# A one-core encoder trunk: input loads issued at once, constants on TensorE first, other banks for k and v, weights through ScalarE's queue, and a smaller share of gathers

## The chip, the core and the metric

One core of a Trainium2 chip runs the whole layer in one launch. Its engines are TensorE (PE; PEld is its loading of stationary operands), VectorE (DVE), ScalarE (ACT), GpSimd (POOL) and SyncE (SP), which issues most transfers. The metric is the device time of one execution, in microseconds (us); the median of several runs counts.

## The reference, cut

One layer over 512 tokens of width 1024: an input projection feeds a differential attention and a two-way gated recurrence (RG-LRU), then a layer with product keys that picks 8 x 16 of 16384 single-neuron experts per token, then a gated embedding, and a last norm.

```python
xn = rms_norm(h, norm_mix_g); proj = xn @ w_in          # q, k, v, lru_in, lru_gate
attn = rms_norm(diff_attention(q, k, v, lam, positions), diff_norm_g)
rec = rms_norm(bi_rglru(lru_in, lru_gate, ...), lru_norm_g)
h = h + concat(attn, rec) @ w_out
xn = rms_norm(h, norm_ffn_g)
ue = exp_u[ib]; logits = einsum('td,tkd->tk', xb, ue)   # 128 experts per token
act = gelu(logits) * gb
ve = exp_v[ib]; h = h + einsum('tk,tkd->td', act, ve)
h = h + sigmoid(rms_norm(h, norm_ple_g) @ ple_w_gate) * (p @ ple_w_proj)
out = rms_norm(h, final_norm_g)
```

## The kernel before

The 512 tokens are four tiles t of 128. Every large product is made of three matmuls (`mm3`, L94): both factors are split into a high and a low part (`split`, L87: ScalarE rounds the high part, L88, VectorE subtracts for the low part, L90 or L92). A scheduler orders each engine's instructions from the order of the code and the waits between them; each engine then runs its own in that order.

**Start.** `x_load` (L183) loads xT in four pieces of two k tiles into `xr`, a ring "w" of three buffers that it shares with the weights; `lru_w` (L175) loads and splits one column tile `ct` of the projection for the recurrence. `x_norm` (L195) loads the four blocks of `h` and takes their squares; `psr` (L278) spreads the resulting `rstd` over the partitions. Then 8 column tiles run over `ct`.

**q, k, v.** The loop at L386 makes three blocks of columns (q, k, v). Each block takes four banks `pst` of the pool `mm` (four buffers), one for each t, so a block can begin only when ScalarE has emptied the banks of the block before (`xn`, L417). Alongside run pieces of the recurrence and its output (`psq`, L360; `psb`, L373; `wo`, L341). After it come the turns `pt` of the attention (L453).

**The experts.** Token tiles 0 to 2 are done densely: the U sweep takes 128 steps over j, each loads a tile of `u`, splits it (`rh`, `rl`) and makes 24 matmuls 128x384 into one of two banks `psl` (`u_mm`, L642), which ScalarE turns into `lg` or, in the last 26 steps, into `keep`. `builds` (L941) makes the matrix of routing weights `gd` in HBM in the background. The V sweep takes 128 steps of 18 matmuls 128x512 into six banks `acc`; its stationary operand is `am` = `lg` times `gc`, the weights of eight steps at a time (`weights`, L981; eight parts a chunk), split into `ah` and `al` (`v_prep`, L1034). `settle` (L989) opens the pools of the V sweep and loads the first chunk of `gc` when the weights are done.

Token tile 3 is done by gathers: 128 rows of `u` and 128 rows of `v`, each one indirect transfer by GpSimd and one VectorE instruction (`rows`, L887; u L913, v L920). `Background.run` paces them: a step gives it a share (`SIDE_1`, `SIDE`, `SIDE_2`, in the V sweep `BG_V`) and a row costs 1.15; what is left runs behind the V sweep. `behind` (L874) places an instruction after the last split made so far.

**End.** `finish(t)` (L1106): norm of `h` (`x`, L1112), turn, split (`hl`), the gate's matmuls (`gate`), sigmoid (L1129), `sg`, `h` (L1130, L1131), last norm (L1141) and store. For t=3 it needs the last gathered row.

Of the kernel before, what the change touches and what calls it, by code (L numbers as in the profile page):

```python
# [39 lines left out]
KEEP = 26  # L40
G_SCALE = 2.0 ** 14
RO_AT = [2, 1, 1, 1, 1, 1, 1, 0, 0, 1, 0, 0, 1, 0, 0, 1, 0, 0, 1, 1, 9]
TOP_FIRST, TOP_THEN, MAKE, SIDE_1, SIDE, BG_V, HOT_DVE, PREP, SIDE_2 = 2.2, 1.0, 0.5, 0.6, 1.2, 1.2, 4, 60, 2.1
LAST = 3
N_AT = 15, 17, 17


# [11 lines left out]
def trunk(ctx, tc, x, xT, pT, pos, w_lru, w_qkv, w_out, w_q, keys, wab, w_gate, w_proj,  # L59
# [85 lines left out]
    with ExitStack() as st:  # L145
# [26 lines left out]
        xgh = ra.tile([P, DK, T], R, name="xgh")  # L172
        xgl = ra.tile([P, DK, T], R, name="xgl")

        def lru_w(ct):  # L175
            w = wr.tile([P, DK, P], F32, tag="w", name="w", bufs=3)
            nc.sync.dma_start(w, w_lru[ct])
            wh = wr.tile([P, DK, P], R, tag="wh", name="wh")
            wl = wr.tile([P, DK, P], R, tag="wl", name="wl")
            split(w, wh, wl)  # L180
            return wh, wl

        def x_load(k2):  # L183
            xr = wr.tile([P, 2, T], F32, tag="w", name="xr", bufs=3)
            nc.sync.dma_start(xr, xT[2 * k2 * P:2 * (k2 + 1) * P, :].rearrange("(k p) t -> p k t", p=P))
            for kk in range(2):
                k = 2 * k2 + kk
                split(xr[:, kk, :], xgh[:, k, :], xgl[:, k, :], scale=col(C_MIX + k))

        x_load(0)  # L190
        wnext = lru_w(0)
        for k2 in range(1, 4):
            x_load(k2)

        def x_norm():  # L195
            for t in range(NT):
# [188 lines left out]

        for blk in range(3):  # L386
            accs = []
            for t in range(NT):
                pst = mm.tile([P, T], F32, tag="mm", name="pst")
                accs.append(pst)  # L390
            for k2 in range(4):
                w2 = wr.tile([P, 2, T], F32, tag="w", name="w2", bufs=3)
# [585 lines left out]
        while feed and len(ahead) < 3:  # L978
            ahead.append(row_load(feed.pop(0)))

    def weights(c, part, vp):  # L981

        if part == 0:
            gcs.append(vp.tile([P, NTB, JC, TB], F32, tag="gc", name="gc"))
        b0, b1 = part * NTB // JC, (part + 1) * NTB // JC
        j = order[c * JC]
        nc.sync.dma_start(gcs[-1][:, b0:b1], gd[b0:b1, :, j * TB:(j + JC) * TB].rearrange("b p (j t) -> p b j t", t=TB))

    def settle():  # L989

        e0.close()
        vp_ = vx.enter_context(tc.tile_pool(name="vp", bufs=2, side="right", reuse_waits="tile"))
        wt_ = wx.enter_context(tc.tile_pool(name="wt", bufs=1, reuse_waits="tile"))
        psv = sv.enter_context(tc.tile_pool(name="psv", bufs=1, space=PSUM, reuse_waits="tile"))
        accs_ = [[psv.tile([P, T], F32, name=f"acc{t}{n}") for n in range(2)] for t in range(ND_V)]
        for part in range(JC):
            weights(0, part, vp_)
        return vp_, wt_, accs_

    vx = ctx.enter_context(ExitStack())  # L1000
# [3 lines left out]
    for j in range(P):  # L1004
# [21 lines left out]
        make.run(MAKE)  # L1026
        if make.done and vp is None:
            vp, wt, acc = settle()
        side.run(SIDE_1 if first else SIDE if not make.done else SIDE_2)
    if vp is None:  # L1030
        make.run(1e9)
        vp, wt, acc = settle()
# [1 line left out]
    def v_prep(i):  # L1034
        j = order[i]
        gj = gcs[i // JC][:, :, i % JC, :]
        lg = kept.get(j)
        if lg is None:
            lg = up.tile([P, NU], F32, tag="lg", name="lg")
            nc.sync.dma_start(lg, ld[j])  # L1040
        if i + JC < P:
            weights(i // JC + 1, i % JC, vp)
        am = vp.tile([P, NTB, TB], F32, tag="am", name="am", bufs=1)
        nc.vector.tensor_mul(am, lg.rearrange("p (b t) -> p b t", t=TB), gj)  # L1044
        am = am.rearrange("p b t -> p (b t)")
        ah = vp.tile([P, NV], R, tag="ah", name="ah", bufs=LAST)
        al = vp.tile([P, NV], R, tag="al", name="al", bufs=LAST)
        split(am, ah, al)
        return ah, al
# [230 lines left out]
```

## Time and profile before

| | us |
|---|---|
| runs | 1506.84, 1513.0, 1511.9 |
| median | 1511.9 |
| the profiled execution, own time | 1509.5 |
| its span | 1507.7 |
| PE busy | 1462.2 |
| DVE busy | 1257.5 |
| ACT busy | 741.0 |

The span is what the engines' rows cover; the profiled execution's own time has 1.8 us more. Rows of a timeline give the start from the span's beginning, the length, the engine, the line, and in brackets how long the engine stood idle before and what ended that. PEclk is the granted clock of TensorE, as a share of the higher of its two levels (1.2 and 2.4 GHz).

### The profile page before, as it was taken

The numbers are of one execution on the slowest core, as the hardware profiler recorded it, in microseconds if no ns is written. First come the engines' busy times: TensorE is split into PE (matmuls) and PEld (weight loads), VectorE is DVE, ScalarE is ACT, GpSimd is POOL, SyncE is SP. The second block draws the span as 40 slices with busy tenths as digits, with TensorE's granted clock in tenths as the row PEclk, the third lists the DMA queues.
The fourth block names the chain that finished last, engine by engine and source line by source line (L and its number), as shares of the span: only waits on it lengthen the run. The fifth ranks groups of instructions, "written<-read, shape, count | busy, mean of one in ns | idle before, by whom it ended". The sixth has DMA issues, their size and how long they took to land.

```text
span 1507.7 us, 22152 instructions
## 1 busy us (share of the span) xinstructions
PE 1462.2 (97%) x7881; PEld 1291.0 (86%) x7881; DVE 1257.5 (83%) x2480; ACT 741.0 (49%) x1058; POOL 414.7 (28%) x320
## 2 busy tenths in 40 slices
PE   7999999999999999999999988999999999999997
PEld 5887668899899999999999986888888778888876
DVE  6686896689999999999778767878897578888896
ACT  6974664253555654565455532333333443333446
POOL 0000000011223263233334344344443014344450
PEclk9999999999999999999999999999999999999999
DMA  7133022157689898889998899989999789999962
GB/s 256 56 98 126 1 74 98 43 185 245 226 288 335 286 355 320 312 296 345 370 331 297 269 323 331 317 299 310 353 363 355 237 274 346 352 375 362 357 211 80
DMA packets 169054, 394.19 MB, mean 261 GB/s; under 512 B 15344, under 2 KB 90864, under 8 KB 165872
## 3 DMA queue, kind: packets, MB, share of 16 engines
q1 hardware_dynamic: 112192, 207.52, 41.0%
q0 software_dynamic: 38464, 140.00, 26.2%
q10 hardware_dynamic: 18288, 45.27, 7.8%
q8 instruction: 61, 1.00, 0.3%
q14 instruction: 49, 0.40, 0.1%
HBM read 345.41 MB, written 47.32 MB: 260 GB/s over the span
## 4 chain that ended last, share of the span: by engine, by line
PE 57%; DVE 20%; DMA 9%; issue 7%; ACT 4%; POOL 1%; SPq 1%; DVEq 0%; ACTq 0%; POOLq 0%
PE psl L95 8%; PE psl L97 8%; PE psl L96 8%; PE acc L97 6%; PE acc L96 6%; PE acc L95 6%; DMA r<-in_v_dram 5%; DVE rl L90 4%; DVE rr L913 2%; PE pg L842 2%; PE ps L95 2%; PE ps L97 2%; PE ps L96 2%; DVE h L920 2%; DMA gc<-gd 1%
## 5 line engine op out<-in xcount | busy, mean ns | idle before, releaser
L88 ACT ACTIVATE rh<-r 128x1024 fp32r<-128x1024 f32 x256 | 270.7, 1059 | 418.2 <-PE psl L96 175.2
L90 DVE TENSOR_TENSOR rl<-r,rh 128x1024 fp32r<-128x1024 f32 x256 | 312.2, 1220 | 103.8 <-ACT rh L88 103.0
L95 PE MATMUL psl<-x2h,rh 128*128 128x384 f32 x1024 | 347.6, 340 | 7.1 <-ACT keep L647 4.7
L97 PE MATMUL psl<-x2h,rl 128*128 128x384 f32 x1024 | 343.7, 336 | 3.1 <-DVE rl L90 3.1
L96 PE MATMUL psl<-x2l,rh 128*128 128x384 f32 x1024 | 343.3, 335 | 0.0
L95 PE MATMUL acc<-rh,ah 128*128 128x512 f32 x768 | 300.0, 391 | 3.4 <-ACT ah L88 3.4
L97 PE MATMUL acc<-rh,al 128*128 128x512 f32 x768 | 300.8, 392 | 1.4 <-DVE al L90 1.4
L96 PE MATMUL acc<-rl,ah 128*128 128x512 f32 x768 | 300.1, 391 | 0.9 <-DVE rl L90 0.9
L881 POOL DMA_INDIRECT rr<-in_u_dram,qidx x84 | 122.3, 1456 | 376.9 <-DVE rl L90 177.0
L95 PEld LDWEIGHTS psl<-x2h,rh 128*128 128x128 f32 x1024 | 192.7, 188 | 8.6 <-ACT keep L647 5.1
L97 PEld LDWEIGHTS psl<-x2h,rl 128*128 128x128 f32 x1024 | 192.8, 188 | 4.0 <-DVE rl L90 4.0
L881 POOL DMA_INDIRECT rr<-in_v_dram,qidxv x82 | 138.9, 1694 | 198.9 <-DVE rl L90 172.9
L96 PEld LDWEIGHTS psl<-x2l,rh 128*128 128x128 f32 x1024 | 192.9, 188 | 0.0
L95 PEld LDWEIGHTS acc<-rh,ah 128*128 128x128 f32 x768 | 145.0, 189 | 33.7 <-ACT ah L88 4.0
L97 PEld LDWEIGHTS acc<-rh,al 128*128 128x128 f32 x768 | 144.8, 189 | 33.5 <-DVE al L90 3.4
L96 PEld LDWEIGHTS acc<-rl,ah 128*128 128x128 f32 x768 | 144.7, 188 | 32.1 <-DVE rl L90 1.8
L88 ACT ACTIVATE ah<-am 128x384 fp32r<-128x384 f32 x128 | 66.3, 518 | 108.3 <-DVE am L1044 84.1
L913 DVE CUSTOM_DVE_ANT_0 rr<-rr,xn 128x1024 f32<-128x1024 f32 x84 | 102.1, 1217 | 5.0 <-DMA rr<-in_u_dram,qidx 5.0
L920 DVE SCALAR_TENSOR_TENSOR h<-rr,qg,h 128x1024 f32<-128x1024 f32 x82 | 104.9, 1280 | 1.4 <-DMA rr<-in_v_dram,qidxv 1.4
L881 POOL DMA_INDIRECT xn<-in_u_dram,qidx x44 | 70.0, 1590 | 112.4 <-DVE rl L90 94.1
L881 POOL DMA_INDIRECT xn<-in_v_dram,qidxv x46 | 72.1, 1568 | 99.5 <-DVE rl L90 91.8
L845 ACT COPY sg<-pg 128x512 f32<-128x512 f32 x96 | 95.9, 1109 | 1.0 <-DMA r<-in_ut_dram 0.2
(340 smaller groups left out, 2271.5 us busy)
## 6 DMA issues: line engine op xcount, KB each, us to landing
r<-in_ut_dram SPq DMA_DIRECT2D x128, 512.0 KB
r<-in_v_dram SPq DMA_DIRECT2D x128, 512.0 KB
gd<-sg ACTq DMA_DIRECT2D x24, 1024.0 KB
gc<-gd SPq DMA_DIRECT2D x128, 192.0 KB
ld<-lg ACTq DMA_DIRECT2D x102, 192.0 KB
lg<-ld SPq DMA_DIRECT2D x102, 192.0 KB
w<-in_w_qkv_dram SPq DMA_DIRECT2D x12, 512.0 KB
w<-in_w_lru_dram SPq DMA_DIRECT2D x8, 512.0 KB
```

The lines of the kernel that those rows point to most:

```text
L88: nc.scalar.activation(hi, src, AF.Copy, scale=1.0 if scale is None else scale)
L90: return nc.vector.tensor_sub(lo, src, hi.bitcast(F32))
L95: nc.tensor.matmul(ps, lhsT=lh, rhs=rh, start=first, stop=False)
L96: nc.tensor.matmul(ps, lhsT=lh, rhs=rl, start=False, stop=False)
L97: nc.tensor.matmul(ps, lhsT=ll, rhs=rh, start=False, stop=last)
L842: nc.tensor.matmul(pg[:, i - q, :], lhsT=o1[:, i // 2, :, i % 2], rhs=o2[part][:, i // 2, :, i % 2], start=part == 0, stop=part == 1)
L845: nc.scalar.copy(sg[:, :, s0:s0 + 4].rearrange("p j t -> p t j"), pg)
L881: g = nc.gpsimd.indirect_dma_start(out=dst, out_offset=None, in_=table, in_offset=bass.IndirectOffsetOnAxis(ap=idx, axis=0))
L913: behind(nc.vector.tensor_tensor_reduce(rr, rr, xn[:, t, :], 1.0, 0.0, ALU.mult, ALU.add, act[:, k % 16:k % 16 + 1]))
L920: behind(nc.vector.scalar_tensor_tensor(h[:, t, :], rr, qg[:, t, k:k + 1], h[:, t, :], op0=ALU.mult, op1=ALU.add))
```

## The change

Five things. (1) `x_load` loads straight into `av`, a tile of its own, and the first column tile's weights come in two halves with two pieces of x behind each; SyncE issues all of it with nothing to wait for. (2) `N_HOT`, 13 matmuls of a constant tile on itself, stand first on TensorE. (3) Two of the banks of k are taken from the pool `psb` ("ro", "po"), and two of v ("tr"). (4) The first chunk of `gc`, eight transfers, is issued by ScalarE, and the first `am` is placed behind the split of V row 2. (5) `SIDE_2`, the share of gathers between `settle` and the end of the U sweep, is 0.6 in the place of 2.1.

```diff
--- before.py
+++ after.py
@@ -40,8 +40,9 @@
 KEEP = 26
 G_SCALE = 2.0 ** 14
 RO_AT = [2, 1, 1, 1, 1, 1, 1, 0, 0, 1, 0, 0, 1, 0, 0, 1, 0, 0, 1, 1, 9]
-TOP_FIRST, TOP_THEN, MAKE, SIDE_1, SIDE, BG_V, HOT_DVE, PREP, SIDE_2 = 2.2, 1.0, 0.5, 0.6, 1.2, 1.2, 4, 60, 2.1
+TOP_FIRST, TOP_THEN, MAKE, SIDE_1, SIDE, BG_V, HOT_DVE, PREP, SIDE_2 = 2.2, 1.0, 0.5, 0.6, 1.2, 1.2, 4, 60, 0.6
 LAST = 3
+N_HOT = 13
 N_AT = 15, 17, 17
 
 
@@ -172,25 +173,32 @@
         xgh = ra.tile([P, DK, T], R, name="xgh")
         xgl = ra.tile([P, DK, T], R, name="xgl")
 
-        def lru_w(ct):
+        def lru_w(ct, parts=1):
             w = wr.tile([P, DK, P], F32, tag="w", name="w", bufs=3)
-            nc.sync.dma_start(w, w_lru[ct])
             wh = wr.tile([P, DK, P], R, tag="wh", name="wh")
             wl = wr.tile([P, DK, P], R, tag="wl", name="wl")
-            split(w, wh, wl)
+            for i in range(parts):
+                c = slice(i * DK // parts, (i + 1) * DK // parts)
+                nc.sync.dma_start(w[:, c, :], w_lru[ct][:, c, :])
+                split(w[:, c, :], wh[:, c, :], wl[:, c, :])
+                if parts > 1:
+                    x_load(2 * i)
+                    x_load(2 * i + 1)
             return wh, wl
 
         def x_load(k2):
-            xr = wr.tile([P, 2, T], F32, tag="w", name="xr", bufs=3)
+
+            xr = av[:, 2 * k2:2 * k2 + 2, :]
             nc.sync.dma_start(xr, xT[2 * k2 * P:2 * (k2 + 1) * P, :].rearrange("(k p) t -> p k t", p=P))
             for kk in range(2):
                 k = 2 * k2 + kk
                 split(xr[:, kk, :], xgh[:, k, :], xgl[:, k, :], scale=col(C_MIX + k))
 
-        x_load(0)
-        wnext = lru_w(0)
-        for k2 in range(1, 4):
-            x_load(k2)
+
+        hot = psb.tile([P, T], F32, tag="tr", name="hot", bufs=2)
+        for _ in range(N_HOT):
+            nc.tensor.matmul(hot[:, 0:P], lhsT=ones, rhs=ones, start=True, stop=True)
+        wnext = lru_w(0, 2)
 
         def x_norm():
             for t in range(NT):
@@ -385,8 +393,13 @@
 
         for blk in range(3):
             accs = []
+
             for t in range(NT):
-                pst = mm.tile([P, T], F32, tag="mm", name="pst")
+                tag = ((), ("ro", "po"), ("tr", None, None, "tr"))[blk][t:t + 1]
+                if tag and tag[0]:
+                    pst = psb.tile([P, T], F32, tag=tag[0], name="pst", bufs=2 if tag[0] == "tr" else 1)
+                else:
+                    pst = mm.tile([P, T], F32, tag="mm", name="pst")
                 accs.append(pst)
             for k2 in range(4):
                 w2 = wr.tile([P, 2, T], F32, tag="w", name="w2", bufs=3)
@@ -978,13 +991,13 @@
         while feed and len(ahead) < 3:
             ahead.append(row_load(feed.pop(0)))
 
-    def weights(c, part, vp):
+    def weights(c, part, vp, queue=nc.sync):
 
         if part == 0:
             gcs.append(vp.tile([P, NTB, JC, TB], F32, tag="gc", name="gc"))
         b0, b1 = part * NTB // JC, (part + 1) * NTB // JC
         j = order[c * JC]
-        nc.sync.dma_start(gcs[-1][:, b0:b1], gd[b0:b1, :, j * TB:(j + JC) * TB].rearrange("b p (j t) -> p b j t", t=TB))
+        queue.dma_start(gcs[-1][:, b0:b1], gd[b0:b1, :, j * TB:(j + JC) * TB].rearrange("b p (j t) -> p b j t", t=TB))
 
     def settle():
 
@@ -994,7 +1007,8 @@
         psv = sv.enter_context(tc.tile_pool(name="psv", bufs=1, space=PSUM, reuse_waits="tile"))
         accs_ = [[psv.tile([P, T], F32, name=f"acc{t}{n}") for n in range(2)] for t in range(ND_V)]
         for part in range(JC):
-            weights(0, part, vp_)
+
+            weights(0, part, vp_, nc.scalar)
         return vp_, wt_, accs_
 
     vx = ctx.enter_context(ExitStack())
@@ -1026,7 +1040,7 @@
         make.run(MAKE)
         if make.done and vp is None:
             vp, wt, acc = settle()
-        side.run(SIDE_1 if first else SIDE if not make.done else SIDE_2)
+        side.run(SIDE_1 if first else SIDE if vp is None else SIDE_2)
     if vp is None:
         make.run(1e9)
         vp, wt, acc = settle()
@@ -1041,7 +1055,10 @@
         if i + JC < P:
             weights(i // JC + 1, i % JC, vp)
         am = vp.tile([P, NTB, TB], F32, tag="am", name="am", bufs=1)
-        nc.vector.tensor_mul(am, lg.rearrange("p (b t) -> p b t", t=TB), gj)
+        mul = nc.vector.tensor_mul(am, lg.rearrange("p (b t) -> p b t", t=TB), gj)
+        if i == 0:
+
+            behind(mul)
         am = am.rearrange("p b t -> p (b t)")
         ah = vp.tile([P, NV], R, tag="ah", name="ah", bufs=LAST)
         al = vp.tile([P, NV], R, tag="al", name="al", bufs=LAST)
```

**ScalarE where the U sweep ends.** The last `gd` write of the matrix of weights, and what follows it. Before:

```order
L847 DMA gd<-sg 128x2048
L88 ACTIVATE rh<-r 128x1024
L647 ACTIVATE keep<-psl 128x384
L88 ACTIVATE rh<-r 128x1024
L647 ACTIVATE keep<-psl 128x384
L88 ACTIVATE rh<-r 128x1024
L647 ACTIVATE keep<-psl 128x384
L88 ACTIVATE ah<-am 128x384
L88 ACTIVATE rh<-r 128x1024
L647 ACTIVATE keep<-psl 128x384
```

Now:

```order
L860 DMA gd<-sg 128x2048
L89 ACTIVATE rh<-r 128x1024
L1000 DMA gc<-gd 128x3x128 x8
L660 ACTIVATE keep<-psl 128x384 x2
L89 ACTIVATE rh<-r 128x1024 x2
L660 ACTIVATE keep<-psl 128x384
L89 ACTIVATE rh<-r 128x1024
L660 ACTIVATE keep<-psl 128x384
L89 ACTIVATE rh<-r 128x1024
L660 ACTIVATE keep<-psl 128x384
L89 ACTIVATE rh<-r 128x1024
```

The eight issues of `gc`, which SyncE had before, stand behind one `rh` and ahead of the next `keep`; `ah` stands behind all of these.

**VectorE at the first `am`.** Before (`ISA` is the u row's product and sum, two rows each):

```order
L90 TENSOR_TENSOR rl<-r,rh 128x1024
L913 ISA rr,act_69<-rr,xn 128x1024
L913 ISA act_69 128x1
L913 ISA rr,act_69<-rr,xn 128x1024
L913 ISA act_69 128x1
L1044 TENSOR_TENSOR am<-lg,gc 128x384
L90 TENSOR_TENSOR rl<-r,rh 128x1024
L913 ISA rr,act_69<-rr,xn 128x1024
L913 ISA act_69 128x1
L90 TENSOR_TENSOR al<-am,ah 128x384
L1044 TENSOR_TENSOR am<-lg,gc 128x384
L90 TENSOR_TENSOR rl<-r,rh 128x1024
```

Now:

```order
L933 SCALAR_TENSOR_TENSOR h<-rr,qg,h 128x1024
L91 TENSOR_TENSOR rl<-r,rh 128x1024 x2
L926 ISA xn,act_69<-xn 128x1024
L926 ISA act_69 128x1
L91 TENSOR_TENSOR rl<-r,rh 128x1024 x2
L926 ISA xn,act_69<-xn 128x1024
L926 ISA act_69 128x1
L91 TENSOR_TENSOR rl<-r,rh 128x1024 x2
L1058 TENSOR_TENSOR am<-lg,gc 128x384
L926 ISA xn,act_69<-xn 128x1024
L926 ISA act_69 128x1
L91 TENSOR_TENSOR al<-am,ah 128x384
```

`am` stood between single splits of rows, with two u rows just ahead of it; now it stands behind a pair of splits that ends with V row 2's, with one u row between the pairs.

**VectorE at the last gathered row** (`h<-rr,qg,h` and `h<-xn,qg,h` are v rows; after the last `rl` of the sweep come 19 of them before and 27 now). Before:

```order
L920 SCALAR_TENSOR_TENSOR h<-rr,qg,h 128x1024
L102 RECIPROCAL sm<-sm 128x1
L920 SCALAR_TENSOR_TENSOR h<-rr,qg,h 128x1024
L1141 SCALAR_TENSOR_TENSOR sg<-h,sm,gains 128x512
L920 SCALAR_TENSOR_TENSOR h<-xn,qg,h 128x1024
L1130 TENSOR_TENSOR sg<-sg,pp 128x512
L1141 SCALAR_TENSOR_TENSOR sg<-h,sm,gains 128x512
L100 TENSOR_SCALAR sm<-sm 128x1
L1131 TENSOR_TENSOR h<-h,sg 128x512
L1130 TENSOR_TENSOR sg<-sg,pp 128x512
L1131 TENSOR_TENSOR h<-h,sg 128x512
```

Now:

```order
L1158 SCALAR_TENSOR_TENSOR sg<-h,sm,gains 128x512
L933 SCALAR_TENSOR_TENSOR h<-rr,qg,h 128x1024
L1147 TENSOR_TENSOR sg<-sg,pp 128x512
L933 SCALAR_TENSOR_TENSOR h<-rr,qg,h 128x1024
L1148 TENSOR_TENSOR h<-h,sg 128x512
L933 SCALAR_TENSOR_TENSOR h<-rr,qg,h 128x1024
L1155 TENSOR_REDUCE sm<-sm 128x1 x2
L933 SCALAR_TENSOR_TENSOR h<-xn,qg,h 128x1024
L101 TENSOR_SCALAR sm<-sm 128x1 x3
L103 RECIPROCAL sm<-sm 128x1 x2
```

Before, two products and sums of gates (`sg<-sg,pp`, `h<-h,sg`) stood behind the last v row; now all those of t=0 to 2 stand ahead of it, and only norms follow until the gates of t=3.

## Rows read from the trace of the kernel before

**Rows 1.** The page, busy us of each engine (share of the span) and its instructions.

```profile
PE 1462.2 (97%) x7881; PEld 1291.0 (86%) x7881; DVE 1257.5 (83%) x2480; ACT 741.0 (49%) x1058; POOL 414.7 (28%) x320
```

**Rows 2.** Windows: stretch, its length, then busy us of PE, PEld, DVE, ACT and POOL with the number of instructions, the granted clock (1.00 is the higher level), the DMA engines' busy share, GB/s.

```profile
116.50:120.00 3.50, 3.50 (x10) 2.73 (x9) 3.50 (x18) 3.50 (x7) 0.00 (x0) 0.52 0.86 276
...
126.50:130.20 3.70, 3.70 (x15) 3.16 (x14) 3.70 (x6) 0.21 (x1) 0.00 (x0) 0.54 0.41 133
...
890.00:900.00 10.00, 5.26 (x23) 4.94 (x22) 7.33 (x12) 3.79 (x6) 3.43 (x3) 0.83 0.84 266
...
917.00:930.00 13.00, 8.15 (x22) 5.77 (x21) 9.65 (x16) 4.93 (x8) 4.90 (x3) 0.74 0.75 259
...
1440.00:1460.00 20.00, 18.83 (x92) 15.46 (x91) 19.44 (x27) 9.18 (x16) 9.47 (x10) 1.00 0.69 215
1460.00:1480.00 20.00, 20.00 (x94) 16.63 (x93) 19.96 (x26) 12.35 (x20) 7.55 (x6) 1.00 0.57 193
```

**Rows 3.** The timeline of the start.

```profile
7.53 0.80 PE L95 MATMUL ps<-xgh,wh 128*128 128x512 f32 x1 [7.53 <-ACT wh L88]
...
13.22 0.63 PE L95 MATMUL ps<-xgh,wh 128*128 128x512 f32 x1
...
14.07 0.40 PE L97 MATMUL ps<-xgh,wl 128*128 128x512 f32 x1
...
19.28 1.06 ACT L198 ACTIVATE gates<-h 128x1024 f32<-128x1024 f32 x1 [0.15 <-DMA h<-in_x_dram]
...
22.26 0.21 ACT L101 ACTIVATE rstd<-rstd 128x4 f32<-128x4 f32 x1
...
23.13 0.71 PE L109 MATMUL psr<-dg,ones 128*128 128x128 f32 x4 [0.57 <-DVE dg L108]
```

**Rows 4.** The timeline between the k and the v block.

```profile
112.35 1.21 DVE L90 TENSOR_TENSOR wl<-w,wh 128x1024 fp32r<-128x1024 f32 x1
...
114.74 2.40 ACT L417 ACTIVATE xn<-pst,rstd 128x512 f32<-128x512 f32 x4
...
115.46 0.50 PE L95 MATMUL pst<-wh,xgh 128*128 128x512 f32 x1 [2.65 <-ACT xn L417]
...
117.37 0.63 PE L95 MATMUL pst<-wh,xgh 128*128 128x512 f32 x1
...
122.62 3.63 PE L360 MATMUL psq<-ones,ugz 128*128 128x2 f32 x32
...
127.92 1.91 PE L453 MATMUL pt<-ident,xn 128*128 128x128 f32 x8
```

**Rows 5.** The waits from 865 to 935: engine and line, what it waited for, us in total, times, longest.

```profile
DVE am L1044 <- DMA r<-in_v_dram: 9.4, 1, 9.4
...
PE psl L95 <- ACT keep L647: 4.7, 1, 4.7
...
PE acc L95 <- ACT ah L88: 3.4, 1, 3.4
```

**Rows 6.** The timelines of ScalarE, SyncE and VectorE where the sweeps meet, one after the other, and SyncE's a chunk later.

```profile
871.65 0.33 ACTq L847 DMA_DIRECT2D gd<-sg  x1
873.69 1.06 ACT L88 ACTIVATE rh<-r 128x1024 fp32r<-128x1024 f32 x1 [2.07 <-PE psl L96]
874.66 0.47 ACT L647 ACTIVATE keep<-psl 128x384 f32<-128x384 f32 x1
878.82 0.47 ACT L647 ACTIVATE keep<-psl 128x384 f32<-128x384 f32 x1
...
893.23 0.52 ACT L88 ACTIVATE ah<-am 128x384 fp32r<-128x384 f32 x1 [9.77 <-DVE am L1044]
...
870.49 14.08 SPq L987 DMA_DIRECT2D gc<-gd  x8
884.66 2.72 SPq L636 DMA_DIRECT2D r<-in_v_dram  x2
...
892.63 0.56 DVE L1044 TENSOR_TENSOR am<-lg,gc 128x384 f32<-128x384 f32 x1 [9.42 <-DMA r<-in_v_dram]
...
930.42 1.97 SPq L987 DMA_DIRECT2D gc<-gd  x4
...
932.96 3.62 SPq L987 DMA_DIRECT2D gc<-gd  x4
```

**Rows 7.** VectorE's timeline around the last v row, then ScalarE's behind that row.

```profile
1474.36 0.68 DVE L1131 TENSOR_TENSOR h<-h,sg 128x512 f32<-128x512 f32 x1
...
1477.48 0.75 DVE L1141 SCALAR_TENSOR_TENSOR sg<-h,sm,gains 128x512 f32<-128x512 f32 x1
1478.14 1.28 DVE L920 SCALAR_TENSOR_TENSOR h<-xn,qg,h 128x1024 f32<-128x1024 f32 x1
1479.34 0.69 DVE L1130 TENSOR_TENSOR sg<-sg,pp 128x512 f32<-128x512 f32 x1
...
1480.62 1.28 ACT L1129 ACT_TABLE_LOAD   x1
1481.92 0.60 ACT L1129 ACTIVATE sg<-gate 128x512 f32<-128x512 f32 x1
```

**Rows 8.** The page's costliest groups: line, engine, operation, tiles, count | busy us, mean ns of one | idle time before them.

```profile
L90 DVE TENSOR_TENSOR rl<-r,rh 128x1024 fp32r<-128x1024 f32 x256 | 312.2, 1220 | 103.8 <-ACT rh L88 103.0
...
L920 DVE SCALAR_TENSOR_TENSOR h<-rr,qg,h 128x1024 f32<-128x1024 f32 x82 | 104.9, 1280 | 1.4 <-DMA rr<-in_v_dram,qidxv 1.4
```

## The prediction

> **What bounds the kernel now.** I read the page's busy shares first [rows 1]: TensorE is busy in 97% of the span, so time is won only where TensorE idles or runs at its lower clock, and lost wherever a new idle stretch opens. Then the windows [rows 2] show where that happens: two dips of the granted clock at the change from the k to the v projection, and two gaps at the meeting of the sweeps (890 to 900: TensorE busy 5.26 of 10 us at 0.83; 917 to 930: 8.15 of 13 at 0.74). The last two windows show another limit: from 1440 to 1480 VectorE is busy 39.4 of 40 us. There the end of the program hangs on VectorE, not on TensorE. The timelines [rows 3, 4, 6, 7] and the waits [rows 5] say who is late in each place. All sums stand against the profiled execution's 1509.5 us; the median of the three runs is 2.4 higher.
>
> **Part 1, the start.** The matmuls of the first column tile take 0.63 us still at 13.22 and 0.40 from 14.07 [rows 3]. A 128x512 matmul takes 0.63 too at 117.37 [rows 4], where the granted clock reads 0.52 [rows 2], so TensorE starts at its lower level, 1.2 GHz, and rises after 6.5 us of work (the first stands at 7.53). Thirteen matmuls on constants before the data could bring that rise forward. But the stretch does not end with these matmuls: `psr` at 23.13 waits for `dg`, that for `rstd` (Sqrt at 22.26), that for the squares of the last x block (19.28). What moves `psr` is when the last block of `h` lands. All input is now issued without the ring of three buffers, 5 MB up to that block as before (four x tiles, two weight tiles, four blocks of `h`, 512 KB each), so it lands somewhat sooner: not at all sooner at worst (gain 0.5, the 0.57 of idle ahead of `psr`), at best 4 (the lower level's cost, 6.5 x (1-0.40/0.63) = 2.4, the 0.57, and 1 by which half a weight tile comes sooner than a whole, an estimate). I take 2.5, since the four squares (1.06 each) still follow one another on ScalarE. Term: -2.5 (-4 to -0.5). If the constants do not raise the clock, nothing else changes, as TensorE then still waits for `psr`.
>
> **Part 2, banks for k and v.** TensorE stood 2.65 us before 115.46, for `xn`, four copies of 2.40 us that empty the banks of k [rows 4]. With other banks it waits for the next `wl` instead, whose split ends at 112.35+1.21 = 113.56: 1.9 us less. After the idle time came 3.5 us at a granted clock of 0.52 [rows 2], that is 1.7 us lost; I count this dip as gone, for the gap falls to 0.75. The second dip (126.5 to 130.2, 0.54, again 1.7) follows 32 tiny `psq` matmuls and a wait for splits; both stay. The eight transposes `pt` that filled that place (1.9) now stand behind the first output matmuls, which cancels against the same work saved later. Term: -3.6. Bounds: -1.5 if the dip comes anyway, -5.5 if the second dip goes too.
>
> **Part 3, the meeting of the sweeps.** What is lost there: 4.74 idle and 1.7 of clock in the first gap, 4.85 and 3.4 in the second, 14.7 us in all [rows 2]. The first is the wait for `keep`, 4.7, and the second for `ah`, 3.4 [rows 5]. Both come from SyncE: its eight `gc` issues hold it from 870.49 for 14.08 us, the first V rows are issued at 884.66, and `am` sits on VectorE in front of the splits that TensorE needs, until 892.63 [rows 6]. The change takes these eight issues to ScalarE's queue and puts the first `am` behind the third V row's split. I count the 14.7 as gone, and add what replaces it.
> (a) The eight issues stand on ScalarE behind `rh` and ahead of `keep` of 874.66. Queued behind them are every `keep` and `rh`. `keep` empties the two psl banks, so TensorE can run one more step, until 878.82, the time of the following `keep`, and then stands until ScalarE is free. Their length is not shown for ScalarE. Nearest rows: the same eight at the same place 14.08; the next eight at 930.42, 1.97+3.62 = 5.59 us. Started at 874.75, where the `rh` of 873.69 ends, they end between 880.3 and 888.8, so the stall is 2 to 10.5, counting 0.5 for `keep`. Since the same transfers run then with fewer gathers beside them, I take 884, a stall of 5.6, and 1.7 of clock behind it, as behind the 4.7 of the first gap.
> (b) At the junction `am` now waits for `rl` of V row 2, whose `rh` needs the buffer of the last U row, so TensorE must have finished the U sweep first: rh 1.06, am 0.56, ah 0.52 [rows 6], rl 1.22 [rows 8], 3.4 us of idle, and 2.5 of clock (1.7 and 3.4 followed the two gaps).
> (c) SyncE still issues seven `gc` of the next chunk ahead of the second V row; I add 2.5 of the old second gap for that (0 to 8).
> Sum: -14.7+7.3+5.9+2.5 = +1 (-9 to +12).
>
> By the Trainium skill, "DMA: Bandwidth & Descriptors", section "Issuing engines are not separate DMA queues", a transfer started by another engine runs on the same 16 engines and interleaves, and moving it saves only the sequencer's issue time, usually small beside the transfer. By that rule (a) would nearly vanish, a total of +2.6 in the place of +9.9. The trace disagrees on the usual smallness: here the issues took 14.08 us [rows 6].
>
> **Part 4, fewer gathers.** SIDE_2 of 0.6 leaves eight rows of token tile 3 undone when the sweeps meet. Counted in the order of VectorE's instructions, 27 v rows follow the last `rl` instead of 19, and three each of the gates' products and sums, and one scaling, now come ahead of the last row. VectorE is full there [rows 2], so each counts: 8 rows at 1.20 (1.28 long, but the instruction behind the row of 1478.14 starts 1.20 after it) = 9.6; three products, three sums and a scaling, 0.69, 0.68 and 0.75 long and 0.08 less each in the same way, 1.8 + 1.8 + 0.7 = 4.3 [rows 7, 8]. The last row moves from 1478.14 by 13.9. Behind it the sigmoid of another tile and its table (1.28+0.60) no longer stand ahead of `x`, of which I count 1.4 as saved, since the table must still be loaded in places. TensorE, which now turns t=3 directly after other gates, will have had no work for over 10 us; after gaps of 2.65 to 4.7 it ran at the lower level for 3.4 us, 1.7 lost, after the second gap 3.4: I add 2.5 to the 13.9 - 1.4. Term: +15 (+12 to +18). The gathers' absence frees some VectorE time near 870 to 885, where it idles anyway (9.4 before `am`), so it is worth nothing beyond part 3.
>
> **Sum.** -2.5-3.6+1+15 = +9.9: 1519.4 for the profiled execution, 1521.8 from the median; I say **1521**.
>
> **Rivals.** *The issues are cheap on ScalarE.* If the eight end by 878.8, (a) is nought: meeting 1-7.3 = -6.3, total +2.6, some 1513, within 0.5%. For it: the second eight took 5.59. Against: the first eight can't read all of gd before its last write, issued at 871.65 [rows 6], has landed. The rule of the Trainium skill quoted in part 3 leads here too. *Faster.* The same mechanism, and the V rows land in time too, (c) 0 and no clock lost at the junction: meeting -14.7+3.4 = -11.3; with the tail at its lower end (+12) and the start and banks at their best (-4, -5.5), -8.8: 1503. It decides at about -7.6. Against it stands the tail: 27 rows of 1.20 cannot be hidden on a full engine. *ScalarE is held as long as SyncE was*, until 888.8: stall 10.5 in place of 5.6, +4.9, and 2 for V rows late after it, total +17: 1529. *The constants do nothing*: 1522 to 1523, since only the first matmuls change.
>
> **How the numbers follow.** A measurement of this kernel tells about 0.5% from no change, that is 1504.3 to 1519.5 counts as the same. Forecast 0.42 (1517 to 1525, some of it under 1519.5); held long 0.13; cheap issues 0.34; faster 0.09; the constants' failure 0.02. Leaving out one in ten below and one above: 1505 to 1531. Faster 0.09, same 0.37, slower 0.54.
>
> **What would show it.** Right: `psr` near 20.6; no TensorE idle time over 1 us between k and v; a TensorE wait of 2 to 10 us for `keep` near 879, with ScalarE's eight `gc` issues before it; 3 to 4 us for `ah` where V starts; no wait near 917; the last v row some 28 us before the end still, with 27 rows after the last `rl`. Wrong: if the wait for `keep` is absent (cheap issues), if a wait for V rows comes back, if VectorE has idle time ahead of the last v row (then part 4 is too large), or if the clock dips in the k/v stretch as before.

## The result, and the profile after

| | before | after |
|---|---|---|
| median of 5 runs | 1512.39 | 1535.59 |
| lowest to highest | 1506.84 to 1517.19 | 1531.33 to 1536.81 |
| the profiled execution | 1509.5 | 1536.38 |
| its span | 1507.7 | 1534.5 |

The ratio is 1.0148, with a 95% interval of 1.0114 to 1.0182: 17 to 28 us slower. The forecast was slower by 9, its range ended at 1531.

The page of the kernel after, busy us of each engine, beside [rows 1]. The work is nearly the same (TensorE's 26 records more are the constants), and the span is longer.

```profile
PE 1470.5 (96%) x7907; PEld 1294.0 (84%) x7907; DVE 1253.2 (82%) x2481; ACT 736.1 (48%) x1057; POOL 387.8 (25%) x320
```

Where the 26.8 us of the two spans lie is seen best between marks that both kernels have, the starts of TensorE's first matmuls of given steps in the trace:

| stretch | before | after | difference | forecast |
|---|---|---|---|---|
| start to the first U matmul | 252.1 | 246.6 | -5.6 | -6.1 |
| U steps 0 to 120 | 605.9 | 606.1 | +0.2 | 0 |
| U step 120 to V step 16 (the meeting) | 116.4 | 117.0 | +0.6 | +1 |
| V steps 16 to 58 | 172.0 | 172.5 | +0.6 | 0 |
| V steps 58 to 124 | 286.0 | 303.1 | +17.1 | 0 |
| V step 124 to the last V matmul | 17.1 | 17.8 | +0.7 | 0 |
| behind it (the tail) | 58.3 | 71.5 | +13.2 | +15 |

One stretch was not in the forecast at all: V steps 58 to 124. The windows of the kernel after (columns as in [rows 2]) show it beside the places that were:

```profile
872.00:880.00 8.00, 0.58 (x4) 0.27 (x2) 0.00 (x0) 0.46 (x2) 0.00 (x0) 0.70 1.13 312
880.00:890.00 10.00, 9.91 (x43) 9.92 (x44) 3.60 (x4) 2.80 (x5) 2.62 (x2) 0.72 0.88 259
...
899.00:903.00 4.00, 0.75 (x4) 0.43 (x3) 2.58 (x3) 1.96 (x3) 1.01 (x1) 0.95 0.44 136
...
1165.00:1180.00 15.00, 7.79 (x32) 5.87 (x32) 6.73 (x9) 5.88 (x8) 1.07 (x2) 0.85 0.78 254
...
1220.00:1260.00 40.00, 35.54 (x145) 27.87 (x145) 28.47 (x38) 17.40 (x23) 8.96 (x8) 0.96 0.78 250
...
1485.00:1506.00 21.00, 14.28 (x64) 11.48 (x62) 21.00 (x26) 10.40 (x19) 10.26 (x8) 0.94 0.69 244
...
120.80:124.40 3.60, 3.60 (x12) 3.02 (x13) 3.57 (x8) 1.72 (x3) 0.00 (x0) 0.53 0.16 23
```

Between k and v (the last row) one dip of the clock is left (0.53), the later of the two of [rows 2]. At the meeting TensorE does nearly nothing from 872 to 880, and for part of the next 10 us it runs at the lower level (0.72). From 1165 to 1180 it is busy 7.79 of 15 us (13.17 in the same window of the kernel before), and from 1220 to 1260 some 4.5 us are idle (0.5 before). From 1485 to 1506 VectorE is busy 21.00 of 21 us, the full engine of [rows 2], now later.

**Start and banks.** The timeline of TensorE, then ScalarE, of the kernel after, in the places of [rows 3]:

```profile
1.15 4.92 PE L200 MATMUL hot<-ones 128*128 128x128 f32 x26 [1.15 <-POOL ones L68]
...
7.52 0.39 PE L98 MATMUL ps<-xgh,wl 128*128 128x512 f32 x1
...
18.02 1.06 ACT L206 ACTIVATE gates<-h 128x1024 f32<-128x1024 f32 x1
...
21.01 0.20 ACT L102 ACTIVATE rstd<-rstd 128x4 f32<-128x4 f32 x1
...
21.87 0.71 PE L110 MATMUL psr<-dg,ones 128*128 128x128 f32 x4 [0.67 <-DVE dg L109]
```

The constants run from 1.15, and the real matmuls take 0.39 from 7.52 on (0.63 still at 13.22 in [rows 3]), but `psr` comes at 21.87 in the place of 23.13: the squares that it needs still come one after the other, the last at 18.02. Between k and v the wait of 2.65 us for `xn` [rows 4] is one of 0.55 for `wl`:

```profile
112.38 0.50 PE L97 MATMUL pst<-wl,xgh 128*128 128x512 f32 x1 [0.55 <-DVE wl L91]
```

**The meeting.** ScalarE's timeline where the sweeps meet, then TensorE's (compare [rows 5, 6]):

```profile
868.29 11.15 ACTq L1000 DMA_DIRECT2D gc<-gd  x8
...
879.54 0.87 ACT L660 ACTIVATE keep<-psl 128x384 f32<-128x384 f32 x2 [10.20 <-DMA gc<-gd]
...
880.09 0.69 PE L96 MATMUL psl<-x2h,rh 128*128 128x384 f32 x1 [7.50 <-ACT keep L660]
...
902.72 0.80 PE L96 MATMUL acc<-rh,ah 128*128 128x512 f32 x1 [3.25 <-ACT ah L89]
```

The eight issues of `gc` hold ScalarE for 11.15 us, `keep` comes at 879.54, and TensorE has stood 7.50 us for it. At the junction it stands 3.25 for `ah`. The wait near 917 is gone.

**V steps 58 to 124.** From V step 60 the kernel prepares the gate's weights (`prepare`, L1076 of the kernel before): twelve transfers, issued by GpSimd (pT, w_proj, w_gate), each split by ScalarE into `wg` and by VectorE. Their target is a buffer of the gathers' ring `rr`:

```python
w = gp.tile([P, D], F32, tag="rr", name="w")
nc.gpsimd.dma_start(w, w_gate[k * P:(k + 1) * P, :])
split(w, wg(k, 0), wg(k, 1))
```

The waits from 1140 to 1262 (columns as in [rows 5]), of the kernel before and then of the kernel after:

```profile
ACT wg L88 <- DMA w<-in_w_gate_dram: 9.8, 5, 4.8
...
ACT wg L88 <- DMA w<-in_w_proj_dram: 5.9, 2, 4.7
...
ACT wg L88 <- DMA w<-in_pT_dram: 5.6, 1, 5.6
...
PE psp L95 <- ACT wg L88: 1.1, 1, 1.1
```

```profile
ACT wg L89 <- DMA w<-in_w_gate_dram: 23.9, 7, 6.4
...
ACT wg L89 <- DMA w<-in_pT_dram: 8.5, 2, 5.0
...
PE psp L96 <- ACT wg L89: 6.8, 1, 6.8
...
ACT wg L89 <- DMA w<-in_w_proj_dram: 5.9, 2, 4.0
```

ScalarE waits 21.3 us for these transfers before and 38.3 after. It runs its instructions in order: while it waits for a weight, the V sweep's own `rh` and `ah` wait behind it, and `psp`, the small product made of the first weights, holds TensorE for 6.8 us in the place of 1.1. In V steps 58 to 124 TensorE is idle for 15.3 us in the place of 2.4; the other 4.2 of the 17.1 are busy time, at a granted clock of 0.98 in the place of 0.99. The reason is on GpSimd. Its timeline from the first of these transfers, of the kernel before and then of the kernel after:

```profile
1153.53 0.61 POOL L1089 DMA_DIRECT2D w<-in_pT_dram  x1
1155.20 1.70 POOL L881 DMA_INDIRECT xn<-in_u_dram,qidx  x1 [1.06 <-DVE rl L90]
1156.91 0.58 POOL L1092 DMA_DIRECT2D w<-in_w_proj_dram  x1
1161.64 0.57 POOL L1089 DMA_DIRECT2D w<-in_pT_dram  x1 [4.16 <-DVE wg L90]
```

```profile
1151.71 0.61 POOL L1106 DMA_DIRECT2D w<-in_pT_dram  x1
1160.78 0.56 POOL L1109 DMA_DIRECT2D w<-in_w_proj_dram  x1 [8.46 <-DVE wg L91]
1167.65 0.54 POOL L1106 DMA_DIRECT2D w<-in_pT_dram  x1 [6.32 <-DVE wg L91]
1174.12 0.53 POOL L1109 DMA_DIRECT2D w<-in_w_proj_dram  x1 [5.92 <-DVE wg L91]
```

Before, a second transfer goes out while the first is under way (1153.53, 1156.91). After, each waits until VectorE has done with the one before: 8.46, 6.32 and 5.92 us idle, released by `wg`. The ring has four buffers `rr`, and the prefetched gathers take turns of four `rr` and three of `xn`. When the preparation begins, gathering stops with five prefetched rows standing; which of the seven buffers they stand in depends on how many rows have been done by V step 60. In the order of GpSimd's instructions the last gathers that can hold buffers through the preparation are two `rr` and three `xn` before, three `rr` and two `xn` after. So eight rows fewer left one free buffer in the place of two, and one transfer in flight in the place of two.

**The tail.** VectorE's last v row of the kernel after, and TensorE's first turn behind it (compare [rows 7]):

```profile
1505.68 1.27 DVE L933 SCALAR_TENSOR_TENSOR h<-xn,qg,h 128x1024 f32<-128x1024 f32 x1
...
1511.19 1.97 PE L1135 MATMUL turn<-ident,x 128*128 128x128 f32 x8 [11.91 <-DVE x L1129]
```

The last row moved from 1478.14 to 1505.68, by 27.5 us. The last V matmul moved by 13.6 of these, lost earlier; from it to the last row there are 14.0 more (forecast 13.9), with 27 rows in the place of 19. Behind the row the end came 0.7 sooner, so the tail as a whole is 13.2 longer. TensorE stood 11.91 us before t=3.

### The profile page after: what moved, and what is told of

It reads as the page before. It is cut to its first block, busy times and chain, and to the rows that moved or that the text cites. A ratio compares the mean times of both kernels' runs of the same rounds, so it can differ in the third digit from the quotient of the medians.

```text
span 1534.5 us, 22155 instructions
## 1 busy us (share of the span) xinstructions
PE 1470.5 (96%) x7907; PEld 1294.0 (84%) x7907; DVE 1253.2 (82%) x2481; ACT 736.1 (48%) x1057; POOL 387.8 (25%) x320
## 5 line engine op out<-in xcount | busy, mean ns | idle before, releaser
L894 POOL DMA_INDIRECT rr<-in_u_dram,qidx x84 | 112.5, 1340 | 396.0 <-DVE rl L91 195.5
L894 POOL DMA_INDIRECT xn<-in_u_dram,qidx x44 | 61.8, 1404 | 139.2 <-DVE rl L91 121.8
L894 POOL DMA_INDIRECT xn<-in_v_dram,qidxv x46 | 64.5, 1402 | 89.1 <-DVE rl L91 80.2
```

Of the source, the lines that this page charges most:

```text
L894: g = nc.gpsimd.indirect_dma_start(out=dst, out_offset=None, in_=table, in_offset=bass.IndirectOffsetOnAxis(ap=idx, axis=0))
```

## The experiments

Each ratio is to runs of the kernel before that were timed beside that kernel (kernels with the same entry under "before" share them), with its 95% interval. The last columns have three stretches of each run's profile, between the marks above.

| run | median | before | ratio | interval | meeting | V 58 to 124 | tail |
|---|---|---|---|---|---|---|---|
| before | 1512.39 | | | | 116.4 | 286.0 | 58.3 |
| after | 1535.59 | 1512.39 | 1.0148 | 1.0114 to 1.0182 | 117.0 | 303.1 | 71.5 |
| e1_share_back | 1511.84 | 1509.64 | 1.0018 | 0.9993 to 1.0042 | 121.8 | 285.3 | 58.2 |
| e2_prep_61 | 1525.69 | 1509.64 | 1.0095 | 1.0068 to 1.0122 | 118.2 | 292.5 | 72.3 |
| e3_before_prep_59 | 1525.45 | 1509.64 | 1.0094 | 1.0065 to 1.0123 | 116.4 | 306.3 | 58.5 |
| e4_share_back_gc_sync | 1504.72 | 1509.64 | 0.9958 | 0.9936 to 0.9979 | 114.2 | 285.9 | 58.2 |
| e5_rows_in_sweep | 1518.01 | 1508.24 | 1.0050 | 1.0033 to 1.0067 | 115.1 | 295.7 | 60.0 |
| e6_gc_gpsimd | 1512.59 | 1508.24 | 1.0020 | 1.0001 to 1.0039 | 119.0 | 285.8 | 58.1 |
| e7_no_constants | 1506.46 | 1508.24 | 0.9976 | 0.9956 to 0.9997 | 113.6 | 284.4 | 58.2 |
| e8_am_early | 1500.34 | 1508.24 | 0.9941 | 0.9920 to 0.9962 | 112.9 | 282.1 | 58.2 |
| e9_share_alone | 1526.36 | 1508.81 | 1.0106 | 1.0070 to 1.0142 | 101.7 | 299.6 | 71.5 |
| e10_banks_alone | 1504.78 | 1508.81 | 0.9978 | 0.9955 to 1.0001 | 112.0 | 284.3 | 58.2 |
| e11_start_and_banks | 1503.61 | 1508.81 | 0.9963 | 0.9940 to 0.9985 | 111.1 | 289.2 | 58.2 |
| e12_prep_68 | 1521.98 | 1508.81 | 1.0079 | 1.0051 to 1.0107 | 113.8 | 287.4 | 72.3 |
| e13_gc_sync_am_early | 1519.98 | 1510.80 | 1.0056 | 1.0035 to 1.0077 | 101.7 | 300.5 | 72.3 |
| e14_gc_sync | 1527.12 | 1510.80 | 1.0104 | 1.0075 to 1.0133 | 105.3 | 303.5 | 71.4 |
| e15_share_rows_back | 1503.45 | 1510.80 | 0.9951 | 0.9928 to 0.9974 | 101.7 | 297.3 | 60.0 |

**e1_share_back.** In the changed kernel:

```diff
-..., BG_V, HOT_DVE, PREP, SIDE_2 = ..., 1.2, 4, 60, 0.6
+..., BG_V, HOT_DVE, PREP, SIDE_2 = ..., 1.2, 4, 60, 2.1
```

> The changed kernel with SIDE_2 back at 2.1, all else kept. Theory 1 (a smaller share costs twice: eight more rows in the tail, +13.2 between the two profiles, and eight rows fewer at V step 60, which leaves the preparation of the gate weights one free buffer in the place of two, +17): both go, 1535.6-13-17 = about 1505 (1502 to 1509), and the stretch from V step 58 to 124 takes what it took before (286 us, not 303). Rival (the preparation is slower because the V sweep meets other transfers after the other parts of the change): only the tail goes, about 1522, and that stretch stays near 303.

Both stretches are back to those of the kernel before, 285.3 and 58.2, so both costs come with the smaller share, and the rival falls. The time itself, 1511.84, came out 7 above the expected 1505: at the meeting ScalarE is now held longer, 16.15 us, and TensorE waits 12.5 us for `keep`. With more gathers beside them the same issues take longer.

**e2_prep_61 and e12_prep_68.** In the changed kernel `PREP = 61`, and `PREP = 68`.

> The changed kernel with the preparation begun at V step 61 in the place of 60, nothing else. Theory 1: one row more is done by then, so the prefetched rows hold two of the four buffers and not three, two weight loads stand in flight, and the 17 us go while the tail's 13 stay: about 1518 (1515 to 1523). Rival (contention, or eight missing rows as such): one step does nothing, about 1535.

> The changed kernel with the preparation begun at V step 68, where as many rows are done as in the kernel before at step 60 (the same two free buffers, the same rows). It tells what is left open by e2_prep_61, which got 6 of the 17 us back by the median and 10.6 by the profile. Theory 1 (buffers alone): as e2_prep_61, 0.9 to 1.0% above the kernel before. Rival (the preparation also depends on which rows are prefetched, which e2 had other than before): all 17 back, 0.2 to 0.5% above the kernel before.

In both, two transfers are in flight, and ScalarE's waits for them fall to 18.7 and 20.3 us. The stretch falls from 303.1 to 292.5 and 287.4, while the tail stays at 72.3: one step in the number at which the preparation begins gives 10.6 us back with the eight rows still missing, so e2's rival (one step does nothing) falls. By the medians it is less: e2 and e12 are 0.5% and 0.7% below the ratio of the changed kernel, 8 and 10 us, and the 1.1% that 17 us would be lies only at the outer ends of the intervals. e2's 1525.69 is also above its theory's range, which ended at 1523. So the direction is shown, and that all 17 us go is not. e12's profile got nearly all back and e2's did not, but e12's median lies between its theory and its rival, and e2's profile is of the slowest of its seven executions (1531.96): whether it matters which rows are prefetched stays open.

**e3_before_prep_59.** In the kernel before, one number:

```diff
-..., PREP, SIDE_2 = ..., 60, 2.1
+..., PREP, SIDE_2 = ..., 59, 2.1
```

> The kernel before with the preparation begun at V step 59 in the place of 60, nothing else. Theory 1: three of the four buffers are held, one weight load is in flight, +17: about 1529 (1523 to 1533), V step 58 to 124 near 303. Rival: within 2 us of the kernel before.

The theory's 1529 was 1525.45, 15.8 above the kernel before, and the stretch took 306.3. Nothing of the change is in this kernel. Its waits from 1140 to 1262:

```profile
ACT wg L88 <- DMA w<-in_w_gate_dram: 20.2, 7, 6.1
...
PE psp L95 <- ACT wg L88: 12.2, 1, 12.2
...
ACT wg L88 <- DMA w<-in_pT_dram: 10.8, 2, 6.3
...
ACT wg L88 <- DMA w<-in_w_proj_dram: 6.6, 2, 3.7
```

They are like those of the kernel after, 37.6 us on ScalarE, with 12.2 on TensorE, and GpSimd's timeline has the same single transfer in flight:

```profile
1155.79 0.60 POOL L1089 DMA_DIRECT2D w<-in_pT_dram  x1
1164.60 0.55 POOL L1092 DMA_DIRECT2D w<-in_w_proj_dram  x1 [8.21 <-DVE wg L90]
```

So the place at which the preparation meets the ring costs this much by itself, with no part of the change there. (The profile is of the slowest of ten executions, 1531.89, so its 306.3 is rather high.) Over all runs the picture is the same: with one free buffer the stretch took 299.6 to 306.3, with TensorE idle for 12.7 to 20.2 us of it (five kernels: after, e3, e9, e13, e14; mean 302.6); with two and BG_V 1.2 it took 282.1 to 292.5, with 1.0 to 6.8 idle (ten kernels, mean 286.3). The means are 16.3 us apart and the groups do not overlap. Within either group single profiles differ by 7 to 10 us, so e2's 292.5 and e12's 287.4 tell no difference. The most direct test, buffers of their own for the weights, was not run.

**e4_share_back_gc_sync, e8_am_early and e6_gc_gpsimd.** On top of e1_share_back, in this order: the issues back on SyncE; that, and `behind(mul)` taken out; the issues on GpSimd (with `behind(mul)`).

```diff
-            weights(0, part, vp_, nc.scalar)
+            weights(0, part, vp_)
...
-        if i == 0:
...
-            behind(mul)
```

> As e1_share_back, and the first chunk of gc issued by SyncE again (the first am still behind V row 2's split). Theory A (what is lost at the meeting in the changed kernel is ScalarE held by the eight issues, a wait of TensorE of 7.7 for keep, and its clock): that wait goes, 4 to 8 us under e1_share_back unless the V rows come late in its place. Theory B (SyncE's hold delays the V rows by as much): the wait moves to the start of the V sweep, within 3 us of e1_share_back or above it.

> As e4_share_back_gc_sync, with the first am no longer placed behind V row 2's split: the banks and the start are then the only parts of the change that are left. Theory (am ahead of the splits holds VectorE and TensorE until the first V row is there): TensorE's losses between 860 and 930 come back to the 16.0 of the kernel before, from 13.8, and the time is 1 to 3 us above e4_share_back_gc_sync, 4 to 5 under the kernel before. Rival (the late am costs at the junction what it saves): the same as e4_share_back_gc_sync within 1 us.

> As e1_share_back, with the first chunk's eight gc transfers issued by GpSimd. Theory (what costs at the meeting is an engine held by the issues: ScalarE 11.2 us in the changed kernel and 16.2 in e1_share_back, SyncE 15.9 in e4_share_back_gc_sync): neither is held, TensorE's waits of 12.7 (e1_share_back) and 6.4 (e4) go, and the 3.4 at the junction stay: 5 to 8 us under e4_share_back_gc_sync, about 1497 to 1500. Rival (the transfers themselves are late: the same bytes through the same 16 DMA engines): the V rows or the weights land as late as before and a wait of 5 or more us stays, 1503 to 1510; GpSimd's gathers queued behind could add to it.

e4 is 0.6% under e1: the hold of ScalarE costs. But SyncE's hold makes the V rows late again (ScalarE stands 11.8 us for the first of them, with `keep` behind it, and TensorE 6.3 for that `keep`), so that 114.2 of the meeting are left. e8 is no slower than e4 without the late `am`: the expectation of 1 to 3 us above e4 fell, as its meeting took 112.9. e6 came out as its rival had it, a wait of more than 5 us that stays (its 1512.59 is even above the rival's range): ScalarE is not held, and the wait moved. Its waits from 865 to 915:

```profile
PE acc L96 <- ACT ah L89: 15.3, 1, 15.3
...
ACT rh L89 <- DMA r<-in_v_dram: 9.8, 1, 9.8
...
DVE rr L926 <- DMA rr<-in_u_dram,qidx: 5.5, 1, 5.5
```

TensorE reached the end of the U sweep without a wait of over 0.5 us and then stood 15.3 us for `ah`, behind V rows and gathers that were late. The third V row was issued only at 888.53, behind seven `gc` of the next chunk on SyncE, and took 17.3 us to land, while gathers that had stood behind GpSimd's own `gc` went out beside it. So at this share a third issuing engine gains nothing; how much of that is the bytes and how much the order of the issues is not told apart. The Trainium skill ("DMA: Bandwidth & Descriptors", "Issuing engines are not separate DMA queues") says that transfers of all issuers run on the same 16 DMA engines and interleave; e6 agrees with that (1.0020, beside 0.9958 with SyncE) but does not prove it. The Trainium skill has it there too that moving them saves only the issue time, usually small beside the transfer; small it was not here, where the issues held ScalarE 11.15 and 16.15 us.

**e9_share_alone.** The kernel before with `SIDE_2 = 0.6`.

> The kernel before with SIDE_2 0.6 in the place of 2.1 and nothing else of the change. Theory 1: eight rows more behind the V sweep (27 for 19), +13, and one free buffer for the preparation, +17 to +20, less up to 5 at the meeting, where fewer gathers share the DMA engines: 25 to 33 us above the kernel before. Rival (the share is harmless by itself and only loses with the other parts): within 8 us of the kernel before.

Both costs are there (299.6, 71.5) and the time is 1.06% up, 17.6 us by the medians and less than the expected 25 to 33, for the meeting gives 14.7 us where up to 5 were expected: 101.7 in the place of 116.4. SyncE's and VectorE's timelines there (compare [rows 6]):

```profile
877.45 9.81 SPq L987 DMA_DIRECT2D gc<-gd  x8
887.36 1.44 SPq L636 DMA_DIRECT2D r<-in_v_dram  x2
...
891.32 0.56 DVE L1044 TENSOR_TENSOR am<-lg,gc 128x384 f32<-128x384 f32 x1 [3.07 <-DMA r<-in_v_dram]
```

The eight issues take 9.81 us in the place of 14.08 on the same SyncE, the V rows go out in time, `am` waits 3.07 in the place of 9.42, and TensorE's waits there are gone but for 0.7 for `sg`. So the smaller share removes the whole loss at the meeting by itself, and some other part of the change brings it back.

**e13_gc_sync_am_early and e14_gc_sync.** The changed kernel with the issues on SyncE: e14; and without the late `am` too: e13.

> The changed kernel with the gc issues on SyncE again and the first am where the order had it (start, constants, banks and the smaller share stay). Theory M (the smaller share frees the DMA engines at the meeting, and ScalarE's hold and the late am cost 15 us there): U step 120 to V step 16 about 102 us, the rest as in the changed kernel (preparation 300, tail 71), about 1518 by the median, 14 under the changed kernel. Rival (the start or the banks shift the transfers so that the meeting is lost anyway): 112 to 117 there, 1530.

> As e13_gc_sync_am_early with the late am kept: the changed kernel with the issues on SyncE alone. Theory M: the late am costs 3.4 of idle time at the junction and its clock, 1.7 to 3.4, the issues on ScalarE the rest: U step 120 to V step 16 about 107, 5 us above e13. Rival (the late am is what brings all of it back): 115 or more.

The meeting took 101.7 in e13, 105.3 in e14 and, with ScalarE, 117.0: the late `am` costs 3.5 us (its wait of 3.3 for `ah`), the issues on ScalarE 11.7. By the medians e13 is 0.9% under the changed kernel and e14 0.4%.

**e7_no_constants, e10_banks_alone and e11_start_and_banks.** e4 without the loop over `N_HOT`; the kernel before with the lines for `tag` alone; e8 without the constants.

> As e4_share_back_gc_sync, without the matmuls on constants. Theory (the end of the start is set by the squares of the last block of h): psr moves by under 0.5 us, the time by under 1. Rival (the constants are what moved psr from 23.1 to 21.5): psr back to about 23, 1.5 to 2 us slower.

> The kernel before with the other banks for k and v and nothing else. Theory (the wait for xn goes, and the clock's dip behind it moves or goes): the first U matmul comes 3.5 to 4.5 us sooner, and the time is 3 to 5 us under the kernel before. Rival (what the banks give, later waits take back): under 1.5 us.

> Only the input at once and the banks: e8_am_early without the constants. Theory (the constants do nothing, since psr ends the start): the same as e8_am_early, 0.4 to 0.8% under the kernel before. Rival (the constants give their 1 to 2 us): 0.1% above that.

TensorE's timeline at the start of e7:

```profile
6.31 0.80 PE L96 MATMUL ps<-xgh,wh 128*128 128x512 f32 x1 [6.31 <-ACT xgh L89]
...
9.40 0.63 PE L96 MATMUL ps<-xgh,wh 128*128 128x512 f32 x1
...
11.89 0.39 PE L96 MATMUL ps<-xgh,wh 128*128 128x512 f32 x1
...
21.33 0.71 PE L110 MATMUL psr<-dg,ones 128*128 128x128 f32 x4 [0.28 <-DVE dg L109]
```

Without the constants the matmuls take 0.63 again, and 0.39 only from 11.89, yet `psr` comes at 21.33, not later than with them (21.87, 21.54 in e4). So the higher clock does not bring the end of the start forward. In time, e4 and e8 with the constants are each 0.2% under e7 and e11 without them; the intervals overlap, so no gain is shown, and a small one is not ruled out.

e10's first U matmul came at 249.9, some 2 sooner than in the kernel before, and not the 3.5 to 4.5 expected, while e9, which changes nothing in that stretch, had it at 256.7: single profiles differ by 4.5 us there. Over all profiles: with the input at once and the banks, thirteen had the first U matmul at 246.0 to 248.8 (mean 247.5); with neither, three (before, e3, e9) at 252.1 to 256.7 (mean 253.9), 6.3 later. And `psr` began at 21.1 to 21.9 in those thirteen (mean 21.4), at 23.1 to 24.3 in the four with the old start (before, e3, e9, e10; mean 23.8). So the start gave about 2.3 us, and the banks about the 4 that are left.

**e5_rows_in_sweep and e15_share_rows_back.** e4 with `BG_V = 1.3`; e11 with `SIDE_2 = 0.6`, `BG_V = 1.28` and `PREP = 61`.

> As e4_share_back_gc_sync, with BG_V 1.3 in the place of 1.2: eleven more rows are done inside the V sweep and 8 are left for the tail in the place of 19 (the preparation still finds two free buffers). Theory T (the tail's price per row holds only where VectorE ends last; at 19 rows TensorE's gates end nearly as late, it stands 1.4 and 1.3 us there): a gain of at most 4 us on e4_share_back_gc_sync, 1500 to 1505, less what the fuller sweep costs. Rival (each row is worth 1.2 to 1.65 us at any count): 11 rows give 13 to 18 us, about 1488 to 1492.

> Input at once and the banks, SIDE_2 0.6, no constants, gc on SyncE, am early, and the eight rows made up inside the V sweep (BG_V 1.28), the preparation at step 61, which leaves it two free buffers. Theory: meeting 102, preparation 286 plus 1 to 5 for the fuller sweep, tail 58: 10 us under e11_start_and_banks by the profile, about 1490 to 1495. Rival (a fuller V sweep loses what the meeting gives, as in e5_rows_in_sweep, 10 us between V steps 58 and 124): 1500 to 1505.

e5: the tail with 8 rows took 60.0, not less than with 19 (58.2), so below 19 the price per row is gone; with 8 rows TensorE's gates end last. The 1518.01 missed both the theory and its rival: V steps 58 to 124 lost 10 us beside e4, though two buffers were free. e15: the meeting's 101.7 and a tail of 60.0 (with 18 rows) together, but 297.3 between. GpSimd's timelines, of e15 and then of e5, show that the preparation began late in both:

```profile
1145.35 1.68 POOL L891 DMA_INDIRECT rr<-in_u_dram,qidx  x1 [1.66 <-DVE rl L91]
1204.08 1.68 POOL L891 DMA_INDIRECT xn<-in_u_dram,qidx  x1 [57.06 <-DVE rl L91]
...
1207.39 0.61 POOL L1100 DMA_DIRECT2D w<-in_pT_dram  x1
```

```profile
1211.89 1.68 POOL L894 DMA_INDIRECT xn<-in_v_dram,qidxv  x1 [59.52 <-DVE rl L91]
1213.58 0.60 POOL L1106 DMA_DIRECT2D w<-in_pT_dram  x1
```

A gather stood 57.06 and 59.52 us for VectorE, and the first weight behind it went out at 1207.39 and 1213.58, not near 1150; `psp` then held TensorE for 6.0 and 4.1 us. So what these two kernels lost there came with a late preparation, and that a fuller sweep costs 10 us as such, as the rival of e15 has it, is not shown. Why the order placed that gather so late is open. e15 is faster than both kernels all the same (0.9951 of the kernel before), as are e4, e7, e8 and e11, and by the intervals none of these five is faster than another.

## Why the prediction was wrong

- **Part 4, the failing step.** "Eight rows undone" was priced in the tail alone, and held "worth nothing beyond part 3" elsewhere. Measured: tail +13.2 (forecast +15), and +17.1 in V steps 58 to 124, a term that the sum did not have. The preparation of the gate weights shares a ring of buffers with the gathers, and a step of its own schedule (V step 60) meets the ring in whatever state the rows done so far have left. e3_before_prep_59 shows that in the kernel before. With that term (16.3 as the mean over the runs) the sum would have been +26, against a measured +23 by the medians and +26.8 by the spans. The tail itself was understood: the last row moved by 14.0 against the last V matmul (forecast 13.9); behind the row 0.7 was saved where 1.1 more was forecast.
- **Part 3, right sum, wrong credit.** Forecast +1, measured +0.6, and the terms hold: the wait for `keep` was put at 5.6 and measured 7.50 (the hold of ScalarE 9.3 and 11.15; both lie between the ends given), the wait at the junction at 3.4 and 3.25. Term (c), 2.5 for V rows behind the next chunk's issues, was not needed; the clock behind the wait for `keep` cost 2.8 (0.72 over 10 us) and not 1.7. But the 14.7 that were counted as gone need no move off SyncE: the smaller share alone removes them (e9_share_alone), and the moves put as much back. At the old share 111 to 122 us stay, with the issues on SyncE, ScalarE or GpSimd.
- **Parts 1 and 2.** -6.1 forecast, -5.6 measured, -6.3 as the mean over the profiles: about 2.3 from the start (forecast 2.5) and 4 from the banks (3.6). That the constants change nothing, given as the argument of part 1, agrees with e7_no_constants and e11_start_and_banks.
- **The signs.** The waits and counts that were named as signs of being right nearly all came: 0.55 us of idle time between k and v, 7.50 for `keep`, 3.25 for `ah`, nothing near 917, 27 rows, 28.8 us behind the last of them; only `psr` was 1.3 late and one dip of the clock stayed. None of them looks at V steps 58 to 124, so they could not warn of the term that was missing.
- **The rivals.** Cheap issues on ScalarE did not come: the lower end, 5.59, was taken from another moment, and at the share of 0.6 the eight issues took 9.81 to 11.77 on either engine. ScalarE was not held as long as SyncE had been either, in this kernel; in e1_share_back, with the old share, it was (16.15). The range failed since every case in it left out the same term.

## What to carry to other kernels

A count of work that moves also moves the phase of every ring of buffers that this work shares: before pricing, list who else allocates from that ring, and look in the order which buffers are held when the other begins. A loop that borrows another's buffers wants buffers of its own, or a start bound to the ring's state (neither was run): here one step was worth 16 us one way (e3) and 8 to 11 the other (e2). When two edits aim at the same loss, time each alone: here the smaller share removed the meeting's 14.7 us, and the edits meant to do the same, ScalarE's queue and the late `am`, put 15 back. And a list of signs should have one for each stretch of the program, also for those that are forecast to stay as they are.

## What the runs showed of the hardware

An issue of a transfer is not short for its engine when many transfers are under way. The same eight `gc` issues, from the start of the first to the end of the last, held SyncE for 13.85 to 15.90 us at the share of 2.1 (eight kernels) and for 9.81 to 11.03 at 0.6 (e9, e13, e14, e15); they held ScalarE for 16.15 at 2.1 (e1) and for 10.50 to 11.77 at 0.6 (after, e2, e12). The hold goes by the gathers beside it far more than by the engine. While an engine is held so, everything behind it in its order waits (10.20 us for `keep` in the kernel after). TensorE's clock, at the lower level for the first 5.6 us of work in e7 and 6.5 in the kernel before, did not set the end of the start: `psr` waits for another chain, and came at 21.33 in e7.
